# A hybrid attention / gated-linear-attention layer: the VectorE and ScalarE instructions of the side work pinned behind the projection product at which they are called

## The chip, the cores and the metric

The kernel runs on one core of one Trainium2 chip. Its engines are TensorE (PE, matrix products; its weight loads are listed as PEld), VectorE (DVE), ScalarE (ACT), GpSimd (POOL) and SyncE (SP, which here issues the loads). Each engine works through its own queue in the order in which the compiler placed the instructions. The metric is the device time of one execution in microseconds, the median of several runs; less is better.

## The reference

One layer (DEPTH 1, batch 1) over 256 latent tokens and 256 context tokens of width 2048, all in float32:

```python
mod_x = split(silu(c) @ w_mod + b_mod, 6);  mod_c = the same of c_ctx
proj = lambda h: project_heads(h, w_in, ...)        # 13,344 columns: qa ka va qb kb vb rb lrf lrb gate_a gate_b
qa, ka, va, qb, kb, vb, rb, gf, gb, gate_a, gate_b = proj(modulate(x, g_mix, mod_x[0], mod_x[1]))
... the same columns of the context, of which keys, values and decays are used
o_attn = windowed_attention(rope(qa), rope(ka), va, context keys and values, sink)   # 16 heads, 4 kv heads, |i-j| <= 128
sf, sb = gla_final_state of the context in both directions                           # GLA: 4 heads, dk 256, dv 512
o_gla  = latent_gla(qb, kb, vb, gf, gb, sf, sb)
x = x + mod_x[2] * merge_branches(o_attn, o_gla, rb, gate_a, gate_b, gla_norm, w_attn_o, w_gla_o, w_out)
x = x + mod_x[5] * conv_ffn(modulate(x, g_ffn, mod_x[3], mod_x[4]), w_up, conv_w, conv_b, w_down)   # D_FF 5632
```

GLA is a linear attention whose state decays per channel by gates made from low-rank columns of the input; it runs over the sequence forwards and backwards and starts from the end states of the context. merge_branches multiplies each branch with the sigmoid of its gate columns. conv_ffn is an up-projection, a depthwise convolution of width 3, SwiGLU, and a down-projection.

## The kernel before

**Products.** Every float32 weight is split in two float32r parts: `split` (L64 to 67) makes `hi` as a rounded copy on ACT and `lo = src - hi` on DVE. A projection is then three products, high x high, high x low and low x high. `proj_nat`, `proj_T` and `proj_pair` walk down the contraction in steps of two 128-row chunks. For each step they call `tick()`, fetch a weight tile of 256 x 512 (`wload`, a 512 KB load by SP into one of 7 buffers with the tag `raw`), split it (`wsplit`: ACT writes `whi`, DVE writes `wlo`, 3 buffers each, traced at high priority) and issue the step's products through `mm` (L73), which remembers the last one in `last[0]`. A step has 24 products where the context goes along (K, V, KA, VA), 12 where only the latent tokens do (QA, RB, gates, `w_attn_o`, `w_gla_o`, `w_out`, `w_down`), and in `proj_pair` (`w_up`) 8 of 512 and 8 of 256 columns.

**Stages.** The opening makes the modulation and the first blocks of Q, K and V, group by group of the contraction; there the order of PE, DVE and ACT is fixed to the program's by `in_order`. Then follow, left to the scheduler: K's second block and the V blocks with one GLA head each beside them, KA and VA (keys and values of the attention), QA four times with the attention of the previous group beside it, RB, the merge (gate columns, `w_attn_o`, `w_gla_o`), `w_out`, and two halves of `w_up` and `w_down`.

**Work beside the projections.** It is called from `tick()`, in three ways:

- `defer(n, fn)`: `fn` runs n + 1 ticks later; used for the transposes of a finished block (`turn`, `to_T`), `second_norm` and others.
- `beside`: a generator, stepped at a rate per tick. `gla_A(h, ...)` (rate 1.65) makes the decay sums (`segs`), and for each of 8 levels a decayed q and k (`q2`, `k2`: ACT exponentials L812 to 820, DVE multiplies L814 and L821, DVE sums L823 to 826), whose small products `pa` come one step later; at the end the context's part with `kf` and `kg` (L844 to 853) and two more steps. `attend(g, ...)` (rate 1.4) does scores, softmax and the product with V.
- `pace()`: background steps at `bg_rate`. After the opening these are the steps of `matvec`, which computes the other four parts of the modulation (`silu(c) @ w_mod`) on DVE: a step takes 256 rows of 512 columns of `w_mod` in a `raw` buffer and adds them, scaled by a column, to `macc` with two multiply-adds (L337, L339). At its call a step issues its own load, if that isn't done, and the next step's. There are 0.3 steps per tick beside the GLA heads, 1.6 in KA and VA, none in QA, 0.52 in RB and the merge, 0.4 in `w_out` and 0.45 in `w_up`.

**What orders this work.** The scheduler simulates the engines when it compiles and places an instruction in its engine's queue when its operands are done by that simulation, oldest call first, splits before all. The products and transposes of the side work have a lower limit beside that: `tick` sets `pin[0] = last[0]`, the last projection product issued, and `mm_b` and `turn_b` (L83, L86) pass their instruction through `after`:

```python
    def after(i):
        if pin[0] is not None:
            tc.add_manual_dep(i.ins, pin[0].name, mybir.DependencyInfo(
                mybir.DependencyClass.NoSync, mybir.DependencyReason.DATA), reason="place among the products")
        return i
```

A NoSync edge keeps the order of placing, without a semaphore. DVE, ACT, POOL and SP have no such limit: their side work is placed as soon as its operands and buffers allow.

Of the kernel before, what the change touches and what calls it, by code (L numbers as in the profile page):

```python
# [30 lines left out]
MODB = [(t, 1) for t in range(4)] + [(t, 2) for t in range(4, 16, 2)]  # L31
DFF = 5632
SCALE = HD ** -0.5


def layer_kernel(ctx, tc, A, out):
    nc = tc.nc
    V, S, G, PE = nc.vector, nc.scalar, nc.gpsimd, nc.tensor
# [36 lines left out]
    def after(i):  # L75

        if pin[0] is not None:
            tc.add_manual_dep(i.ins, pin[0].name, mybir.DependencyInfo(
                mybir.DependencyClass.NoSync, mybir.DependencyReason.DATA), reason="place among the products")
        return i  # L80

    def mm_b(*a, **k):
        return after(PE.matmul(*a, **k))  # L83

    def turn_b(*a):
        return after(PE.transpose(*a))  # L86
# [800 lines left out]
    def v_block(c0, name):  # L887
        vh, vl = M(name + "h", [P, 4, 512], F32R), M(name + "l", [P, 4, 512], F32R)
        proj_nat(w_in, 0, c0, ALL, h_xc, lambda i, b: split(vh[:, i, :], vl[:, i, :], b))
        return vh, vl  # L890
# [22 lines left out]
    def with_gla(h, kb, block):  # L913
        res = []
        beside[:] = [gla_A(h, kb, qbt, res), 1.65, 0.0]
        v = block()
        for _ in beside[0]:
            pass
        beside.clear()
        return res, v  # L920
# [6 lines left out]
    a, kb1 = with_gla(0, kbt, kb_block)  # L927
# [4 lines left out]
    for h in (1, 2, 3):  # L932
        a, v = with_gla(h, kb1 if h > 1 else kbt, lambda h=h: v_block(VB + h * 512, f"v{h}"))
# [77 lines left out]
    def attend(g, qT):  # L1011
# [3 lines left out]
        for t in range(2):  # L1015
# [14 lines left out]
            sk = sink[:, 4 * g:4 * g + 4]  # L1030
            V.scalar_tensor_tensor(mx, mx, SCALE, sk, op0=ALU.mult, op1=ALU.max)
            V.tensor_tensor(es, sk, mx, op=ALU.subtract)
            V.tensor_scalar(mx, mx, -1.0, None, op0=ALU.mult)
            S.activation(es, es, AF.Exp)
            for h in range(4):
                S.activation(sc[h], sc[h], AF.Exp, scale=SCALE, bias=mx[:, h:h + 1],  # L1036
                             accum_out=ds_[:, h:h + 1])
# [306 lines left out]
```

## Time and profile before

| | |
|---|---|
| median of 3 runs | 2018.4 us (2017.47 to 2019.22) |
| the profiled execution's own time | 2015.55 us |
| its span, first to last instruction | 2013.3 us |
| mean granted TensorE clock | 0.999 |
| HBM read | 413.48 MB |

Times in the profile are microseconds from the start of the span, unless marked ns. A row of a group gives line, engine, operation, the tiles as output<-inputs, the shapes, the count, then busy time, mean ns of one, and the idle time of the engine before them with what ended it. L73 is the projections' products, L83 and L86 the side work's products and transposes, L66 and L67 the two halves of a split, L106 the loads. A row of the waits reads: who waited, for whom, us in total, times, the longest. A row of the timeline reads: start, length, engine, line, operation, tiles, count, and in brackets the idle time before it. A matmul's end is modelled, and products overlap in the pipeline, so that their lengths add up to more than the time between their starts.

### The profile page before, as it was taken

What the parts mean: (1) busy time and instruction counts of PE and PEld (TensorE: products, weight loads), DVE (VectorE), ACT (ScalarE), POOL (GpSimd) and SP (SyncE); (2) the same over time, 40 slices, a digit from 0 to 9 for tenths busy, and PEclk for the clock granted to TensorE, in tenths of its full rate; (3) what the DMA queues carried; (4) which work ended last, traced back from release to release, by engine and by line L of the source; (5) the groups of instructions that cost most, each with busy time, mean ns of one, the idle gap of its engine ahead of it and who ended that gap; (6) DMA issues with size and microseconds to landing.
All of it is one profiled execution on the core that took longest, in us unless ns stands there. A gap on an engine that the chain in (4) does not pass through costs nothing.

```text
span 2013.3 us, 27564 instructions
## 1 busy us (share of the span) xinstructions
PE 1985.8 (99%) x10452; PEld 1649.7 (82%) x10452; DVE 1447.0 (72%) x2246; ACT 970.6 (48%) x1415; POOL 37.2 (2%) x56
## 2 busy tenths in 40 slices
PE   9999999999999999999999999999999999999998
PEld 7778888887777777887778888888888888888887
DVE  5656767887758888877776476899897455667754
ACT  5223565552345656444344445665555434555532
POOL 0001000001000000000000000000000000000000
PEclk9999999999999999999999999999999999999999
DMA  9876222346543456788887586588885655555563
GB/s 390 330 274 218 92 83 86 102 125 205 171 156 116 129 187 203 254 278 270 272 272 239 189 313 209 179 267 270 265 273 199 211 197 189 188 188 188 189 215 110
DMA packets 200437, 417.41 MB, mean 207 GB/s; under 512 B 13040, under 2 KB 13456, under 8 KB 195696
## 3 DMA queue, kind: packets, MB, share of 16 engines
q1 hardware_dynamic: 198816, 411.48, 61.3%
q0 software_dynamic: 1056, 4.08, 0.6%
q8 instruction: 82, 1.34, 0.3%
q14 instruction: 51, 0.42, 0.1%
q10 hardware_dynamic: 432, 0.09, 0.0%
HBM read 413.48 MB, written 2.11 MB: 206 GB/s over the span
## 4 chain that ended last, share of the span: by engine, by line
PE 58%; DMA 5%; DVE 3%; issue 1%; ACT 0%; DVEq 0%; ACTq 0%
PE acc L73 43%; PE accs L73 12%; DMA raw<-in_w_mod 5%; DVE macc L339 2%; DVE wlo L67 1%; PE poa L83 1%; PE pS L83 1%; PE ptp L86 1%; PE pto L86 0%; ACT whi L66 0%; PE ptx L86 0%; DVE s L1041 0%; ACT s L1036 0%; DVE macc L337 0%; PE ptq L86 0%
## 5 line engine op out<-in xcount | busy, mean ns | idle before, releaser
L66 ACT ACTIVATE whi<-raw 128x1024 fp32r<-128x1024 f32 x536 | 567.5, 1059 | 701.3 <-PE acc L73 493.7
L67 DVE TENSOR_TENSOR wlo<-raw,whi 128x1024 fp32r<-128x1024 f32 x536 | 653.7, 1223 | 294.9 <-ACT whi L66 269.1
L339 DVE SCALAR_TENSOR_TENSOR macc<-raw,ccol,macc 128x512 f32<-128x512 f32 x240 | 181.0, 754 | 104.5 <-DMA raw<-in_w_mod 101.1
L73 PE MATMUL acc<-h,whi 128*128 128x512 f32 x672 | 183.8, 395 | 0.0
L73 PE MATMUL accs<-h,whi 128*128 128x512 f32 x672 | 180.3, 390 | 0.0
L73 PEld LDWEIGHTS accs<-h,whi 128*128 128x128 f32 x672 | 126.2, 188 | 28.2
L73 PE MATMUL acc<-whi,ah 128*128 128x512 f32 x352 | 137.1, 389 | 0.0
L73 PE MATMUL acc<-whi,al 128*128 128x512 f32 x352 | 137.1, 389 | 0.0
L73 PE MATMUL acc<-whi,h00hi 128*128 128x512 f32 x336 | 134.1, 399 | 0.5 <-DVE val L67 0.5
L73 PE MATMUL acc<-whi,h01hi 128*128 128x512 f32 x336 | 133.6, 398 | 0.0
L73 PE MATMUL acc<-whi,h00lo 128*128 128x512 f32 x336 | 131.9, 393 | 0.0
L73 PE MATMUL acc<-whi,h01lo 128*128 128x512 f32 x336 | 131.7, 392 | 0.0
L73 PEld LDWEIGHTS acc<-h,whi 128*128 128x128 f32 x672 | 115.6, 190 | 15.1
L73 PEld LDWEIGHTS acc<-h,wlo 128*128 128x128 f32 x672 | 102.7, 189 | 13.1
L73 PE MATMUL accs<-h,wlo 128*128 128x256 f32 x672 | 108.0, 283 | 0.0
L73 PE MATMUL acc<-h,wlo 128*128 128x256 f32 x672 | 106.8, 282 | 0.0
L73 PE MATMUL acc<-wlo,ah 128*128 128x512 f32 x352 | 94.1, 389 | 0.0
L73 PE MATMUL acc<-wlo,h01hi 128*128 128x512 f32 x336 | 93.0, 395 | 0.8 <-DVE wlo L67 0.7
L73 PE MATMUL acc<-wlo,h00hi 128*128 128x512 f32 x336 | 93.5, 393 | 0.1
L73 PEld LDWEIGHTS accs<-h,wlo 128*128 128x128 f32 x672 | 92.7, 192 | 0.0
L73 PEld LDWEIGHTS acc<-wlo,ah 128*128 128x128 f32 x352 | 66.1, 188 | 13.7
L73 PEld LDWEIGHTS acc<-whi,ah 128*128 128x128 f32 x352 | 66.1, 188 | 13.7
(406 smaller groups left out, 3668.0 us busy)
## 6 DMA issues: line engine op xcount, KB each, us to landing
raw<-in_w_in SPq DMA_DIRECT2D x204, 512.0 KB, 4.3
raw<-in_w_up SPq DMA_DIRECT2D x184, 512.0 KB, 3.5
raw<-in_w_mod SPq DMA_DIRECT2D x128, 512.0 KB, 4.2
raw<-in_w_down SPq DMA_DIRECT2D x88, 512.0 KB, 3.6
mraw<-in_k_wm SPq DMA_DIRECT2D x32, 1024.0 KB, 8.7
raw<-in_w_attn_o SPq DMA_DIRECT2D x32, 512.0 KB, 5.1
raw<-in_w_gla_o SPq DMA_DIRECT2D x32, 512.0 KB, 4.7
raw<-in_w_out SPq DMA_DIRECT2D x32, 512.0 KB, 4.7
```

What stands on the lines that cost most here:

```text
L66: S.activation(hi, src, AF.Copy)
L67: V.tensor_tensor(lo, src, hi.bitcast(F32), op=ALU.subtract)
L73: last[0] = PE.matmul(*a, **k).ins
L83: return after(PE.matmul(*a, **k))
L86: return after(PE.transpose(*a))
L339: V.scalar_tensor_tensor(a[0], raw[:, k, :], vec[:, kt:kt + 1], a[0], op0=ALU.mult, op1=ALU.add)
```

## The change

`V` and `S`, by which the kernel calls VectorE and ScalarE, become wrappers that pass each instruction through `after`. Whatever is called inside `tick()` (deferred functions, the generators, the background steps) gets the edge to the last projection product; outside `tick()` `pin[0]` is None and nothing changes. So evacuations at the end of a projection, `wsplit`, and what is left of a generator after its block have no new edge. Loads by SP, POOL's instructions, and `nc.scalar.dma_start` have none either. No instruction is added or removed.

```diff
+class Placed:
+
+
+    def __init__(self, engine, place):
+        self.engine, self.place = engine, place
+
+    def __getattr__(self, name):
+        f = getattr(self.engine, name)
+
+        def call(*a, **k):
+            return self.place(f(*a, **k))
+
+        return call
+
+
 def layer_kernel(ctx, tc, A, out):
     nc = tc.nc
     V, S, G, PE = nc.vector, nc.scalar, nc.gpsimd, nc.tensor
...
         return i
+
+    V = Placed(V, after)
+    S = Placed(S, after)
 
     def mm_b(*a, **k):
         return after(PE.matmul(*a, **k))
```

## The prediction

> **What bounds the kernel now.** I read the page first (busy shares, the chain that ended last), then the windows of 50 us, then who waits for whom, then the timeline at the longest waits.
>
> ```profile
> span 2013.3 us, 27564 instructions
> ...
> PE 1985.8 (99%) x10452; PEld 1649.7 (82%) x10452; DVE 1447.0 (72%) x2246; ACT 970.6 (48%) x1415; POOL 37.2 (2%) x56
> ...
> PE acc L73 43%; PE accs L73 12%; DMA raw<-in_w_mod 5%; DVE macc L339 2%; DVE wlo L67 1%; PE poa L83 1%; PE pS L83 1%; PE ptp L86 1%; PE pto L86 0%; ACT whi L66 0%; PE ptx L86 0%; DVE s L1041 0%; ACT s L1036 0%; DVE macc L337 0%; PE ptq L86 0%
> ```
>
> TensorE is busy for 99% of the span, so no change to VectorE or ScalarE can win more than the places where a product has to wait. The chain names one foreign cause: loads of w_mod, their multiply-adds `macc`, and `wlo` behind them. Where that lies is seen in the windows (columns: stretch, length, busy time and count of PE, PEld, DVE, ACT, POOL, clock, DMA share, GB/s):
>
> ```profile
> 900.00:950.00 50.00, 47.56 (x212) 38.16 (x211) 37.34 (x49) 20.23 (x21) 0.00 (x0) 1.00 0.81 269
> 950.00:1000.00 50.00, 48.89 (x210) 38.37 (x209) 35.76 (x45) 19.03 (x19) 0.00 (x0) 1.00 0.83 277
> 1000.00:1050.00 50.00, 48.51 (x215) 38.65 (x214) 37.20 (x47) 20.23 (x21) 0.00 (x0) 1.00 0.80 265
> 1050.00:1100.00 50.00, 49.91 (x221) 40.23 (x220) 35.06 (x47) 20.08 (x20) 0.00 (x0) 1.00 0.75 254
> 1100.00:1150.00 50.00, 50.00 (x226) 41.38 (x225) 24.58 (x23) 21.27 (x22) 0.00 (x0) 1.00 0.58 190
> ```
>
> From 900 to 1100 us PE is idle 2.44 + 1.11 + 1.49 + 0.09 = 5.1 us; in the window after it, where `macc` has ended, not at all, at one product per 50 / 226 = 0.221 us. The waits (total us, times, longest):
>
> ```profile
> PE acc L73 <- DVE wlo L67: 4.7, 7, 1.6
> PE pa L83 <- DVE q L814: 3.0, 4, 0.9
> PE pa L83 <- DVE kf L852: 2.5, 4, 1.0
> PE po L83 <- DVE v3l L67: 2.5, 1, 2.5
> PE ptk L86 <- DVE sq L972: 1.9, 1, 1.9
> ...
> DVE macc L339 <- DMA raw<-in_w_mod: 101.1, 58, 3.6
> ...
> PEld acc L73 <- DVE wlo L67: 11.1, 15, 2.0
> ```
>
> VectorE stands still 101.1 us for w_mod rows that haven't landed, with `wlo` splits queued behind it. One case, on four engines (start, length):
>
> ```profile
> 925.52 0.37 SPq L106 DMA_DIRECT2D raw<-in_w_mod  x1
> ...
> 929.23 1.06 ACT L66 ACTIVATE whi<-raw 128x1024 fp32r<-128x1024 f32 x1 [1.66 <-PE acc L73]
> ...
> 930.74 1.54 DVE L339 SCALAR_TENSOR_TENSOR macc<-raw,ccol,macc 128x512 f32<-128x512 f32 x2 [2.85 <-DMA raw<-in_w_mod]
> ...
> 932.20 1.22 DVE L67 TENSOR_TENSOR wlo<-raw,whi 128x1024 fp32r<-128x1024 f32 x1
> ...
> 933.47 1.20 PE L73 MATMUL acc<-wlo,oh 128*128 128x512 f32 x4 [1.56 <-DVE wlo L67]
> ```
>
> The load is issued at 925.52 and its `macc` starts only at 930.74, 5.2 us later; VectorE idled 2.85 us for it, then spent 1.54, and the product waited 1.56 us for the `wlo` behind.
>
> **The change part by part.** Every V and S call made inside `tick()` gets a no-sync edge to the last projection product. Such an edge puts no wait on the chip; it only forbids the compiler to place the instruction in its engine's queue ahead of that product. Three kinds of work are touched.
>
> (1) `macc` (L337, L339) and its transposes. Nothing is added or removed; their places move back past the `wlo` splits of about two later chunks (the `whi`/`wlo` tiles have three buffers). How far ahead they run now: RB's weights and half a `matvec` step per tick share the 7 `raw` buffers, and each step runs as soon as its load lands. Held back, a step's load lands several ticks of 12 x 0.221 = 2.7 us before its place, against the 5.2 us above, so the 2.85 us kind of idle goes and `wlo` is late by 1.54 us of work at most, which its lead over PE covers. What is late next is PE itself. Size: the 7 gaps sum to 4.7 us, but a product is shown busy longer than its pace, so each wait hides a little more:
>
> ```profile
> L73 PE MATMUL acc<-whi,ah 128*128 128x512 f32 x352 | 137.1, 389 | 0.0
> ```
>
> 0.389 - 0.221 = 0.17 us per wait, over the 15 waits that the weight loads show: 4.7 + 15 x 0.17 = 7.2 us. Bounds: 4.7 from the gaps alone; from the counts, 4 x 226 - (212 + 210 + 215 + 221) = 46 products too few, 46 x 0.221 = 10.2 us (too much, as the windows differ in their small products). I take 7.2, since it is built on the waits themselves.
>
> [...]
>
> Two single stalls have the same cause. At the end of the fourth GLA head and in the attention:
>
> ```profile
> 464.27 2.49 DVE L339 SCALAR_TENSOR_TENSOR macc<-raw,ccol,macc 128x512 f32<-128x512 f32 x3
> ...
> 466.67 1.48 DVE L67 TENSOR_TENSOR wlo<-raw,whi 128x1024 fp32r<-128x1024 f32 x1
> ...
> 468.07 2.47 DVE L67 TENSOR_TENSOR v3l<-acc,v3h 128x512 fp32r<-128x512 f32 x4
> ...
> 468.80 0.50 PE L83 MATMUL po<-v3l,ats 128*128 128x512 f32 x1 [2.52 <-DVE v3l L67]
> ```
> ```profile
> 740.38 1.54 DVE L339 SCALAR_TENSOR_TENSOR macc<-raw,ccol,macc 128x512 f32<-128x512 f32 x2 [2.49 <-DMA raw<-in_w_mod]
> ...
> 742.58 0.50 PE L83 MATMUL poa<-ptl,vah 128*128 128x512 f32 x1 [0.88 <-DVE ptl L67]
> ```
>
> The first: three multiply-adds of steps that belong to KA's ticks stand ahead of the split that the `po` products need. KA's first steps are pinned to the last V product, so one or two may still stand there: between 0 and 2.5 us gone, I take 1.5. The second: 0.9 us gone with its DMA wait.
>
> Cost on SP's queue: a `raw` buffer with w_mod rows is now held until its tick, so later loads, which are issued in order, start later. In KA and VA (1.6 steps per tick of 24 x 0.221 = 5.3 us) the 7 buffers hold about 5 w_mod tiles and one or two weight chunks; in RB and the merge (0.52 steps per tick) two or three w_mod tiles and four chunks. One buffer's cycle, from the rows
>
> ```profile
> raw<-in_w_mod SPq DMA_DIRECT2D x128, 512.0 KB, 4.2
> ...
> L66 ACT ACTIVATE whi<-raw 128x1024 fp32r<-128x1024 f32 x536 | 567.5, 1059 | 701.3 <-PE acc L73 493.7
> L67 DVE TENSOR_TENSOR wlo<-raw,whi 128x1024 fp32r<-128x1024 f32 x536 | 653.7, 1223 | 294.9 <-ACT whi L66 269.1
> ```
>
> is 4.2 + 1.06 + 1.22 = 6.5 us: 1.2 buffers needed in VA, 2.4 in the merge. Covered, in VA barely.
>
> Cost on VectorE's queue in VA. The last KA/VA step runs at 526.77 to 535.69 now; its tick is VA's last, before `vah` at 567:
>
> ```profile
> 535.69 0.75 DVE L339 SCALAR_TENSOR_TENSOR macc<-raw,ccol,macc 128x512 f32<-128x512 f32 x1
> ...
> L66 ACT ACTIVATE vah<-acc x4: 576/592/610, 567.0 to 568.5; 128x512 fp32r<-128x512 f32 x4
> ...
> 500.00:550.00 50.00, 48.06 (x218) 38.71 (x217) 36.24 (x77) 16.22 (x28) 0.00 (x0) 1.00 0.56 179
> 550.00:600.00 50.00, 49.45 (x221) 40.33 (x220) 25.71 (x42) 20.27 (x28) 0.00 (x0) 1.00 0.46 140
> ```
>
> Some six ticks' steps, 6 x 1.6 x 1.5 = 14 us of VectorE, move into 530 to 567, where by these windows 28 to 49% of 37 us, 10 to 18 us, is free. Queued behind them are `val` and the key transposes, for which PE waits. I add 1.5 us; bounds 0 and 5 (three steps of 1.5 us ahead of `val`).
>
> (2) `gla_A`'s exponentials, multiplies and sums, which today may run a level ahead of their tick. They are now made in the tick whose products (or the next tick's) read them. PE's waits on them today are the eight above, 5.5 us. They may go (-5.5), or the other 4 x 7 = 28 level groups may wait likewise, 5.5 / 8 = 0.7 us each (+19.6). Today's groups already follow their operand closely without a gap:
>
> ```profile
> 308.76 0.69 DVE L821 TENSOR_TENSOR k<-k,kb 128x512 f32<-128x512 f32 x1
> ...
> 309.60 1.13 PE L83 MATMUL pa<-q,k 128*128 128x128 f32 x8
> ```
>
> (operand done 309.45, product 309.60, no idle), so I stay near zero: +1.5 us for two late groups.
>
> (3) All else at nothing. `attend`'s and the deferred turns' V and S work reads products that are pinned to the same tick already. In the opening each engine's order is fixed by hand. `second_norm` feeds `h2`, first read a block side later (8 ticks). POOL's `gc` sums and gate transfers follow pinned products' ACT work as before. The up stage shows no wait on `wlo` today: there `macc` waits are covered by 2 chunks' lead.
>
> Sum: -7.2 - 1.5 - 0.9 + 1.5 + 1.5 = -6.6 us: span 2013.3 to 2006.7, the profiled execution 2015.55 to 2008.95; that execution lies 2.85 us under the median, so the median goes from 2018.4 to 2011.8.
>
> **Rivals.** *Nothing measurable*: the edges bind only at compile time, and where VectorE's order keeps `macc` ahead of the same `wlo`, or costs (1) and (2) eat the gain, the time stays 2018.4. For it: all gains hang on some 17 waits. Against: 101 us of DMA wait in one queue should not survive a move of several ticks.
>
> *Operands just in time* (slower): without the level in hand each level's product is placed when the compiler thinks its operands are done, and the chip is 0.7 us late at all 28: +19.6 - 9.6 = +10.0, 2028.4. It decides from 14 late groups (9.6 / 0.7). Against it the row at 309.60; for it the eight waits, at the head's first and last groups.
>
> *Ring too short* (slower): every KA/VA chunk's load waits for held steps: 6.5 + 1.5 - 5.3 = 2.7 us a tick, 16 ticks, less two chunks in hand (10.6): +32.6, with the 8.1 us from elsewhere 2042.9. It decides when less than 1.2 buffers are left. [...]
>
> *More than counted*: counts' size and the eight waits too, -10.2 - 2.5 - 0.9 - 5.5 = -19.1: 1999.3.
>
> **How the numbers follow.** Forecast 0.48 (its own range 2007 to 2015), nothing 0.25, just in time 0.13, ring 0.06, more 0.08. A measurement of this kernel tells about 0.2% or 4 us from no change. Faster: 0.45 of the forecast's 0.48 + 0.08 = 0.53; same 0.25 + 0.03 = 0.28; slower 0.19. The range 2003 to 2026 leaves out "more", the ring and half of "just in time", 0.2 in all.
>
> **What would show it.** Right: `macc`'s wait for w_mod falls from 101 us to under 20; the `acc` from `wlo` row (4.7) all but goes; windows 900 to 1100 show 225 products each; the last w_mod `macc` of that stretch starts 20 us or more later than now. Wrong: the `pa` rows grow above 10 us, `whi` waits for weight loads, or VA's window shows PE idle before `vah`'s successors.

## The result and the profile after

| | before | after |
|---|---|---|
| median (runs) | 2017.93 us (2015.10 to 2019.22, 4) | 2004.20 us (2003.26 to 2004.61, 4) |
| the profiled execution's own time | 2015.55 us | 2004.46 us |
| its span | 2013.3 us | 2002.6 us |
| predicted | | 2011.8 us (2003 to 2026) |

The ratio is 0.9933, 95% interval 0.9916 to 0.995: faster by 0.7%, which is clear of the noise. The time lies at the lower end of the stated range and under the 2007 to 2015 us that the forecast had for itself, nearer to the rival "more than counted" (1999.3). The spans differ by 10.7 us, the medians by 13.7. The difference between the two is where the profiled execution of before lies among its own runs: 2.4 us under their median, in a spread of 4.1 us.

The page of the kernel after, its first lines and the chain by line. The wrapper now issues every VectorE and ScalarE instruction, so these all carry its line, L46; products of the projections are L88, those of the side work L101, turns L104.

```profile
span 2002.6 us, 27556 instructions
...
PE 1980.9 (99%) x10452; PEld 1651.1 (82%) x10452; DVE 1446.1 (72%) x2246; ACT 970.0 (48%) x1415; POOL 34.7 (2%) x56
...
PE acc L88 47%; PE accs L88 12%; PE pto L104 0%; PE ptx L104 0%; PE pcl L101 0%; DVE yd L46 0%; DVE wlo L46 0%; PE pr L101 0%; DVE u L46 0%; DVEq L1357 0%; DVE al L46 0%; DVE gcol L46 0%; PE pt_gate L104 0%; DVEq L46 0%
```

The loads of w_mod, 5% of the chain before, and `macc`, 2%, are gone from it. PE's busy share says nothing: 99% both times, and the same 10452 products. The windows say more (columns as before):

```profile
500.00:550.00 50.00, 46.54 (x210) 36.80 (x208) 38.86 (x83) 13.53 (x26) 0.00 (x0) 1.00 0.61 191
550.00:600.00 50.00, 49.08 (x215) 40.06 (x216) 37.00 (x56) 22.28 (x30) 0.00 (x0) 1.00 0.73 236
900.00:950.00 50.00, 50.00 (x227) 41.22 (x226) 40.77 (x52) 21.04 (x23) 0.00 (x0) 1.00 0.86 291
950.00:1000.00 50.00, 50.00 (x223) 40.91 (x222) 39.05 (x51) 20.39 (x21) 0.00 (x0) 1.00 0.82 279
1000.00:1050.00 50.00, 50.00 (x226) 41.13 (x225) 39.75 (x53) 20.89 (x22) 0.00 (x0) 1.00 0.85 291
1050.00:1100.00 50.00, 50.00 (x226) 41.12 (x225) 34.44 (x41) 20.95 (x23) 0.00 (x0) 1.00 0.73 253
```

From 900 to 1100 us PE has no idle time left, and 902 products stand where 858 stood. From 500 to 600, in VA, there are 425 where there were 439: this stage became slower. The waits, of all engines, and the group of `macc`:

```profile
ACT whi L46 <- DMA raw<-in_w_in: 72.4, 21, 6.7
ACT whi L46 <- DMA raw<-in_w_up: 42.8, 27, 3.6
...
PE pa L101 <- DVE kf L46: 2.8, 4, 0.9
...
PE pa L101 <- DVE q L46: 2.4, 4, 0.9
```
```profile
L46 DVE SCALAR_TENSOR_TENSOR macc<-raw,ccol,macc 128x512 f32<-128x512 f32 x240 | 179.7, 749 | 2.1
```

`macc` waits for no load any more (2.1 us of idle time before all 240 of them, against 104.5 us before, 101.1 of them behind loads). In its place the first half of a split, `whi`, waits for weights: 72.4 us for w_in and 42.8 us for w_up, two rows that before did not have. No row of `acc` behind `wlo` is left on PE.

Where the 10.7 us lie is read by counting the products of the projections (tiles acc, accs, acx) in both traces and comparing the start of the same product. Each cell is what a stretch became longer or shorter, in us; all experiments are set against the same profile of before:

| products (us in the trace before) | after | macc only | all but macc | resident | short | VA 0.8 | 0.45 | lead 2 | 6 buffers | lead 2, 0.8 | lead 4 | lead 12 | before, 6 |
|---|---|---|---|---|---|---|---|---|---|---|---|---|---|
| to the 1800th (428) | 0.0 | -1.3 | +1.0 | +8.9 | +0.7 | -0.1 | 0.0 | +0.1 | +2.3 | +1.0 | -0.5 | +0.1 | +3.4 |
| to the 2000th (494), end of the fourth head | -3.5 | +2.2 | -4.2 | -1.7 | +0.6 | -3.7 | -2.1 | -2.0 | -3.7 | -2.1 | -2.1 | -1.8 | +2.5 |
| to the 2400th (591), VA | +2.7 | +2.0 | -0.3 | -2.2 | +2.4 | -2.9 | +3.4 | -2.2 | +2.7 | -3.0 | -2.2 | +2.9 | -0.3 |
| to the 3400th (894), attention, RB | -0.6 | 0.0 | +0.4 | -0.5 | +1.6 | 0.0 | +2.9 | -1.6 | +6.5 | -0.2 | -0.9 | +5.6 | +2.8 |
| to the 4200th (1088), merge | -9.3 | -9.3 | -0.4 | -9.3 | -9.3 | -8.9 | -0.9 | -9.3 | +8.2 | -8.9 | -9.3 | -3.7 | -0.1 |
| to the last | 0.0 | 0.0 | +3.4 | 0.0 | 0.0 | +0.4 | +4.5 | 0.0 | +16.1 | +0.4 | 0.0 | 0.0 | +1.6 |
| sum | -10.7 | -6.3 | 0.0 | -4.9 | -4.0 | -15.2 | +7.8 | -15.1 | +32.2 | -12.7 | -15.0 | +3.2 | +9.9 |

One column is one execution. How far two executions of the same order lie apart is seen in three of them. The kernel with 0.45 steps has the instructions of before on PE, VectorE and ScalarE in the same order up to 717 us, and its stretches there still differ by -2.1 and +3.4 us. The kernels with all edges but `macc`'s and with twelve ticks ("lead 12") have the order of before throughout the merge (824 instructions on PE, 173 on VectorE, 79 on ScalarE), and their merges differ by -0.4 and -3.7 us. So a single cell of 2 or 3 us says little; what comes back in several kernels says more. The merge's -9.3 comes back to a tenth of a microsecond in five other kernels.

The case that the prediction showed at 925 us, now (start, length):

```profile
912.25 0.37 SPq L124 DMA_DIRECT2D raw<-in_w_mod  x1
...
925.87 1.23 DVE L46 TENSOR_TENSOR wlo<-raw,whi 128x1024 fp32r<-128x1024 f32 x1 [0.83 <-ACT whi L46]
927.01 1.53 DVE L46 SCALAR_TENSOR_TENSOR macc<-raw,ccol,macc 128x512 f32<-128x512 f32 x2
...
927.29 1.07 PE L88 MATMUL acc<-wlo,h01hi 128*128 128x512 f32 x4
```

`wlo` stands ahead of the two multiply-adds, which start without a wait, and the products behind `wlo` start without one. The second multiply-add is the first to read the load issued at 912.25, which landed at 915.79. Counted step by step, in the merge of before the first multiply-add of each of the 31 steps starts 0.0 to 0.8 us after its load has landed, and 28 of them have waited for it: VectorE comes to nearly every load before it is there. In the kernel after it is 9.6 to 17.2 us behind the landing (34 steps), and none waits.

### The profile page after: what moved, and what is told of

The parts are those of the page before. It is cut to its first block, busy times and chain, and to the rows that moved or that the text cites. A ratio compares the mean times of both kernels' runs of the same rounds, so it can differ in the third digit from the quotient of the medians.

```text
span 2002.6 us, 27556 instructions
## 1 busy us (share of the span) xinstructions
PE 1980.9 (99%) x10452; PEld 1651.1 (82%) x10452; DVE 1446.1 (72%) x2246; ACT 970.0 (48%) x1415; POOL 34.7 (2%) x56
## 4 chain that ended last, share of the span: by engine, by line
PE 60%; DVE 0%; DVEq 0%; issue 0%
PE acc L88 47%; PE accs L88 12%; PE pto L104 0%; PE ptx L104 0%; PE pcl L101 0%; DVE yd L46 0%; DVE wlo L46 0%; PE pr L101 0%; DVE u L46 0%; DVEq L1357 0%; DVE al L46 0%; DVE gcol L46 0%; PE pt_gate L104 0%; DVEq L46 0%
## 5 line engine op out<-in xcount | busy, mean ns | idle before, releaser
L46 ACT ACTIVATE whi<-raw 128x1024 fp32r<-128x1024 f32 x568 | 601.6, 1059 | 765.9 <-PE acc L88 455.8
L46 DVE TENSOR_TENSOR wlo<-raw,whi 128x1024 fp32r<-128x1024 f32 x568 | 694.5, 1224 | 383.9 <-ACT whi L46 353.6
L88 PE MATMUL acc<-h,whi 128*128 128x512 f32 x672 | 183.9, 395 | 0.0
L46 DVE SCALAR_TENSOR_TENSOR macc<-raw,ccol,macc 128x512 f32<-128x512 f32 x240 | 179.7, 749 | 2.1
L88 PE MATMUL accs<-h,whi 128*128 128x512 f32 x672 | 180.3, 390 | 0.0
L88 PEld LDWEIGHTS accs<-h,whi 128*128 128x128 f32 x672 | 126.2, 188 | 28.2
L88 PE MATMUL acc<-whi,ah 128*128 128x512 f32 x352 | 137.2, 390 | 0.0
L88 PE MATMUL acc<-whi,al 128*128 128x512 f32 x352 | 137.1, 389 | 0.0
L88 PE MATMUL acc<-whi,h00hi 128*128 128x512 f32 x336 | 134.3, 400 | 2.0 <-ACT y L46 1.4
L88 PE MATMUL acc<-whi,h01hi 128*128 128x512 f32 x336 | 133.8, 398 | 2.3 <-ACT whi L46 2.3
L88 PE MATMUL acc<-whi,h00lo 128*128 128x512 f32 x336 | 131.9, 393 | 0.0
L88 PE MATMUL acc<-whi,h01lo 128*128 128x512 f32 x336 | 131.6, 392 | 0.0
L88 PEld LDWEIGHTS acc<-h,whi 128*128 128x128 f32 x672 | 115.6, 190 | 15.1
L88 PEld LDWEIGHTS acc<-h,wlo 128*128 128x128 f32 x672 | 102.8, 189 | 13.1
L88 PE MATMUL accs<-h,wlo 128*128 128x256 f32 x672 | 108.0, 283 | 0.0
L88 PE MATMUL acc<-h,wlo 128*128 128x256 f32 x672 | 106.8, 282 | 0.0
L88 PE MATMUL acc<-wlo,ah 128*128 128x512 f32 x352 | 94.1, 389 | 0.0
L88 PE MATMUL acc<-wlo,h00hi 128*128 128x512 f32 x336 | 93.7, 394 | 0.0
L88 PEld LDWEIGHTS accs<-h,wlo 128*128 128x128 f32 x672 | 92.8, 192 | 0.0
L88 PE MATMUL acc<-wlo,h01hi 128*128 128x512 f32 x336 | 92.7, 393 | 0.0
L46 DVE SCALAR_TENSOR_TENSOR u<-us,cols,u 128x255 f32<-128x255 f32 x176 | 77.6, 478 | 0.5
L88 PEld LDWEIGHTS acc<-wlo,ah 128*128 128x128 f32 x352 | 66.1, 188 | 13.7
```

The lines of the kernel that those rows point to most:

```text
L46: return self.place(f(*a, **k))
L88: last[0] = PE.matmul(*a, **k).ins
```

## The experiments

The theory after the result: in the merge, `wlo` stood in VectorE's queue behind a `macc` whose load had not landed; places moved back end that. Open were which edges matter, whether the wait or the work of `macc` is the harm, and what VA's loss comes from.

**One part alone.** The edges on `matvec`'s four VectorE instructions only, on top of the kernel before:

```diff
-                    V.scalar_tensor_tensor(a[0], raw[:, k, :], vec[:, kt:kt + 1], a[0],
+                    after(V.scalar_tensor_tensor(a[0], raw[:, k, :], vec[:, kt:kt + 1], a[0],
...
-                V.tensor_reduce(rs, tr, op=ALU.add, axis=AX.X)
+                after(V.tensor_reduce(rs, tr, op=ALU.add, axis=AX.X))
```

> The kernel before, with the edge to the last product only on the VectorE instructions of matvec (multiply-adds, transpose, reduction). If the whole gain is matvec's (theory): span 2002.6 +- 1.5 us, as after: 9.3 us less between 900 and 1085 us, about 3.5 less at 450 to 475, about 2.8 more in VA. If the edges on the GLA heads' exponentials and multiplies had a part (rival), the span differs from 2002.6 by more than 2 us, with the difference between 200 and 470 us.

And the change without these, so with all other edges:

```diff
-                    V.scalar_tensor_tensor(a[0], raw[:, k, :], vec[:, kt:kt + 1], a[0],
+                    nc.vector.scalar_tensor_tensor(a[0], raw[:, k, :], vec[:, kt:kt + 1], a[0],
...
```

> The changed kernel without the edges on matvec's VectorE instructions. Theory: nothing happens, span 2013.3 +- 1.5 us, macc still waits about 100 us for w_mod loads, and the acc products wait about 4.7 us for wlo. Rival (edges on the GLA heads matter): 2 us or more to either side, found between 200 and 470 us.

Measured: the first 2007.81 us, ratio 0.9952 (0.9936 to 0.9968); the second 2013.34 us, 0.9981 (0.997 to 0.9992). The two ratios multiply to 0.9933, that of the change. The theory that all is `matvec`'s missed: the first kernel's span is 2007.0 us and not 2002.6. The second's span came out as said, 2013.3 us, but by luck, as -4.2 and +3.4 us cancel in it; its ten runs are faster than before by 0.2%. The merge's 9.3 us belong to `matvec`'s edges alone: with all others the waits stay as before:

```profile
DVE macc L357 <- DMA raw<-in_w_mod: 106.0, 61, 3.7
...
PE acc L88 <- DVE wlo L46: 8.2, 13, 2.3
```

The end of the fourth head goes the other way: -4.2 us without `matvec`'s edges, +2.2 with them alone. Its gain belongs to the edges on `gla_A`: the four kernels that hold `gla_A` to its own tick show -3.5 to -4.2 us there, and those without such edges, before among them, between -2.1 and +2.5. The size is therefore anything from 1.4 us up. Taking `macc` away from ahead of the split does not end the stall. The first `po` products, in the kernel with `matvec`'s edges alone, in the one without them, and in the kernel after:

```profile
460.83 1.03 PE L83 MATMUL pa<-q,kg 128*128 128x256 f32 x4
...
467.24 0.84 PE L83 MATMUL po<-v3h,ats 128*128 128x512 f32 x2 [1.97 <-ACT v3h L66]
```
```profile
465.03 1.03 PE L101 MATMUL pa<-q,kg 128*128 128x256 f32 x4
...
466.82 0.39 PE L101 MATMUL po<-v3h,ats 128*128 128x512 f32 x1
```
```profile
461.40 0.68 DVE L46 TENSOR_TENSOR v3l<-acc,v3h 128x512 fp32r<-128x512 f32 x1
...
464.30 1.03 PE L101 MATMUL pa<-q,kg 128*128 128x256 f32 x4
...
466.33 0.40 PE L101 MATMUL po<-v3h,ats 128*128 128x512 f32 x1
```

With `gla_A` held, the `pa` products of its context part (`kg`) stand 3.5 to 4.2 us later than with `matvec`'s edges alone, and one of the four `v3` splits (two in the second kernel) is made ahead of the weights' split (461.40), so `po` has operands at once.

**Wait or work.** In the kernel before, `macc` reads a constant tile that is always there; the loads, their count and the time on VectorE stay:

```diff
-                    V.scalar_tensor_tensor(a[0], raw[:, k, :], vec[:, kt:kt + 1], a[0],
+                    V.scalar_tensor_tensor(av, ov, vec[:, kt:kt + 1], av,
                                            op0=ALU.mult, op1=ALU.add)
```

> The kernel before, where matvec's multiply-adds read a tile that is always there instead of the loaded rows; the loads are still issued (the modulation's four later parts are thus not computed). No edges. VectorE's work and its size stay, the wait for the load goes. If the wait is what delays wlo: PE idle from 900 to 1100 us falls from 5.1 to under 1 us, span near 2004. If the 1.5 us of work ahead of wlo is what delays it: PE idle stays at 4 to 5 us.

And the reverse: it still waits for its load, but works on 32 of 512 columns:

```diff
-                    V.scalar_tensor_tensor(a[0], raw[:, k, :], vec[:, kt:kt + 1], a[0],
+                    V.scalar_tensor_tensor(a[0][:, 0:32], raw[:, k, 0:32], vec[:, kt:kt + 1], a[0][:, 0:32],
                                            op0=ALU.mult, op1=ALU.add)
```

> The kernel before, where matvec's multiply-adds cover 32 of 512 columns (the modulation's four later parts are thus not computed in full): they still wait for their load, but take about 0.1 us instead of 0.75. If the wait is what delays wlo: PE still idles 3 us or more from 900 to 1100 us. If the work is: under 1 us.

Measured: 2010.57 and 2011.07 us, one time each. Both free the merge wholly, PE 50.00 in each of the four windows, by the same 9.3 us. (The resident one loses 8.9 us in the opening, where a product waits 3.73 us for `kb`.) The short one does so while VectorE waits for w_mod longer than before in the whole kernel, and nearly as long in the merge (40.1 us against 45.1):

```profile
DVE macc L339 <- DMA raw<-in_w_mod: 136.1, 71, 6.0
```
```profile
900.00:950.00 50.00, 50.00 (x227) 41.21 (x226) 32.73 (x52) 21.28 (x22) 0.00 (x0) 1.00 0.88 293
...
1050.00:1100.00 50.00, 50.00 (x224) 41.18 (x223) 29.80 (x42) 20.67 (x21) 0.00 (x0) 1.00 0.68 223
```

So neither the wait nor the work is the harm by itself: `wlo`'s lead over PE covers each, and not both one after the other. The theory of the wait alone missed here. The short kernel is the firmer half of this: VectorE's order in its merge is nearly that of before (162 of 173 instructions match in sequence), while in the resident one, which has no load to wait for, the compiler orders the queue anew (103 of 173).

**Fewer steps.** The kernel before with 0.45 instead of 0.52 steps per tick in RB and the merge, to see whether the stall is set by the rate of the loads:

```diff
-    bg_rate[0] = 0.52
+    bg_rate[0] = 0.45
```

> The kernel before, without edges, with 0.45 matvec steps per tick in RB and the merge instead of 0.52. In the trace before, w_mod loads follow each other at about 6.1 us (986.64 - 918.15 over 11), each issued only after the previous step's macc and wlo; PE at full speed would call one every 2.84 / 0.52 = 5.5 us. If that closed loop bounds the merge (theory): at one every 2.84 / 0.45 = 6.3 us PE no longer waits, and most of the 9.3 us between 900 and 1085 goes, span 2004 to 2006. If each step just costs its own delay (rival): 9.3 x 0.45 / 0.52 = 8.0 us stay, span 2012.

Measured: 2020.93 us, ratio 1.0025 (1.0013 to 1.0037), where the theory had 2004 to 2006 us and the rival 2012. The waits did not shrink, and the trace shows +4.5 us after the merge. That the steps left over delay the stages behind is likely but not shown, as the kernel with all edges but `macc`'s, whose order there is nearly that of before, shows +3.4:

```profile
DVE macc L339 <- DMA raw<-in_w_mod: 127.4, 63, 5.1
...
PE acc L73 <- DVE wlo L67: 7.5, 11, 1.9
```

The theory of a loop closed through the buffers, which a lower rate would open, falls. What fits is that each step carries its own risk of a delay, wherever it is put: in this kernel's merge, too, 29 of 30 steps come to their load before it has landed.

**What VA's loss is.** Two cures of different kinds. Fewer held steps, 0.8 instead of 1.6 per tick in KA and VA:

```diff
-    bg_rate[0] = 1.6
+    bg_rate[0] = 0.8
```

> The changed kernel with 0.8 matvec steps per tick in KA and VA instead of 1.6 (the rest of the steps runs on in the merge at the same 0.52). If VA's 2.8 us come from held steps (buffers and VectorE's time): PE's waits there (whi 2.3, y 1.4 us) go, the span is 2002.6 - 2.8 = 1999.8 +- 1 us. If they come from the edges themselves or the evacuation of KA: unchanged, 2002.6 +- 1.

The same steps, held less long, by an edge to the projection product two ticks earlier:

```diff
+LEADT = 2
...
+    def after_early(i):
+        if pin[0] is not None and early[0] is not None:
+            tc.add_manual_dep(i.ins, early[0].name, mybir.DependencyInfo(
...
-    V = Placed(V, after)
-    S = Placed(S, after)
+    V = Placed(V, after_early)
+    S = Placed(S, after_early)
...
+        past.append(last[0])
         pin[0] = last[0]
+        early[0] = past[max(0, len(past) - 1 - LEADT)]
```

> The changed kernel with the VectorE and ScalarE edges on the projection product of two ticks earlier. If what counts is that macc is placed after its load has landed: the merge keeps its 9.3 us (the load is issued four to six ticks ahead), and VA loses less than 2.8 us, as buffers are freed two ticks sooner; span 2000 to 2003. If macc must stand behind the split of its own tick: half of the merge's waits return, 2007.

Measured: 2000.98 us, ratio 0.9922 (0.9907 to 0.9937), and 2000.03 us, 0.9918 (0.9902 to 0.9935). The first has a span of 1998.1 us, under the 1999.8 +- 1 that was expected. Both turn VA's +2.7 into a gain, -2.9 and -2.2. That +2.7 is no larger than what two executions of before differ by (the kernel with 0.45 steps has +3.4 there, with a 3.8 us wait of `ptk` for `sq`); but the change swaps that stall for another, and the medians point the same way, 3.2 and 4.2 us under the change's, though the intervals of the ratios overlap. The stall in the kernel after is a load that comes late:

```profile
525.14 0.37 SPq L124 DMA_DIRECT2D raw<-in_w_in  x1
531.40 2.91 SPq L124 DMA_DIRECT2D raw<-in_w_mod  x2
538.28 0.37 SPq L124 DMA_DIRECT2D raw<-in_w_in  x1
```
```profile
541.69 1.06 ACT L46 ACTIVATE whi<-raw 128x1024 fp32r<-128x1024 f32 x1 [5.46 <-DMA raw<-in_w_in]
...
542.79 0.50 PE L88 MATMUL acc<-whi,h01hi 128*128 128x512 f32 x1 [1.27 <-ACT whi L46]
```

The weights' load is issued at 538.28, 13.1 us after the weights' load before it and behind two loads of w_mod, for which a buffer has to come free. From 480 to 592 us SP waits 24.9 us for a `macc` to free one, against 15.2 in before, 17.0 with two ticks and 2.8 with 0.8 steps. With the edge two ticks earlier the 72.4 us that `whi` waits for w_in are 8.3, and PE's window is full:

```profile
ACT whi L47 <- DMA raw<-in_w_in: 8.3, 5, 2.1
```
```profile
500.00:550.00 50.00, 50.00 (x230) 40.59 (x229) 43.46 (x88) 16.21 (x29) 0.00 (x0) 1.00 0.65 211
550.00:600.00 50.00, 49.07 (x218) 39.69 (x217) 32.98 (x52) 21.15 (x29) 0.00 (x0) 1.00 0.61 197
```

VectorE is busier there (43.46 us) than in the kernel after (38.86), and PE doesn't mind: VA's loss is weight loads that come late, and not VectorE's work.

**The ring.** The change with 6 `raw` buffers, and the kernel before with 6:

```diff
-wr = pool(name="wr", bufs=7)
+wr = pool(name="wr", bufs=6)
```

> The changed kernel with 6 raw buffers instead of 7. If the ring is what VA lacks: VA's cost grows from 2.8 to more than 5 us, with whi waiting on w_in loads for well over 72 us in all, while the merge (2.4 buffers needed for weights) stays without waits; span 2005 to 2010. If VectorE's time is what VA lacks: 2002.6 +- 1.

> The kernel before with 6 raw buffers instead of 7. If holding the steps is what makes the ring short (the kernel with the change lost 43 us at 6 buffers), the kernel before, which frees a buffer as soon as its load has landed, loses less than half of that: 2018 to 2038 us, with whi waiting on loads of w_up, where no step runs, as long as there. Rival, that 6 buffers are too few for the weights by themselves: 2055 to 2065 us, whi waiting on loads over 200 us.

Measured, one time each: the change 2047.22 us, 43 us above its own median with 7; the kernel before 2025.46 us, beside a median of 2016.85. In the change the weights wait for loads in every stage with steps, and PE with them:

```profile
ACT whi L46 <- DMA raw<-in_w_in: 133.5, 58, 7.5
ACT whi L46 <- DMA raw<-in_w_up: 80.5, 48, 4.9
...
PE acc L88 <- ACT whi L46: 26.9, 30, 2.8
```

In the kernel before with 6 the longest waits for loads are still those of `macc`, not of `whi`:

```profile
DVE macc L339 <- DMA raw<-in_w_mod: 108.1, 61, 3.9
...
ACT whi L66 <- DMA raw<-in_w_out: 6.2, 3, 4.3
```

So 6 buffers are nearly enough for the work itself; it is holding the steps that needs the seventh. (I had expected `whi` of before to wait for w_up as long as in the change, as if no step ran there; it waits 2.9 us for it against 80.5, and 71.6 of these fall before 1540 us, where steps still run.) My size for the change with 6 (2005 to 2010 us) was far too small, and its place was wrong: VA's cost did not grow, +2.7 us as with 7, with `whi` waiting 38.8 us for loads there against 43.7. The merge, which was to stay without waits, lost 17.5 us against the change with 7, and the stages behind it 16.1. Why a buffer less does no harm in VA is left open.

**How late is late enough.** The edge to the product four and twelve ticks earlier (10.6 and 32 us ahead in the merge), and the two cures of VA together:

> The change with edges on the product four ticks earlier (10.6 us ahead in the merge, 21 us in VA). If an instruction does harm only when it is queued before its load has landed: a load takes 4 to 7 us to land, and it is issued only when a buffer is free, so the merge keeps most of its 9.3 us and the time is 2000 to 2003 us, with macc waiting on loads 10 to 40 us. Rival, that the two ticks were the whole margin: waits of acc on wlo come back, 2 to 5 us, and 2004 to 2008 us.

> The change with edges on the product twelve ticks earlier (32 us in the merge, 64 us in VA), where the edges hardly bind. If place alone matters, the merge goes back to the kernel before: macc waits on loads 80 to 100 us, acc on wlo 3 to 5 us, 3 to 9 us of the merge's gain gone, 2009 to 2014 us; the end of the fourth head loses its 3.5 us too. Rival, that the merge's gain comes from some other effect of the edges (another order of the splits): it stays, 2000 to 2004 us.

> The change with edges on the product two ticks earlier and 0.8 instead of 1.6 steps of matvec per tick in KA and VA. Theory that both cures mend one and the same cost (VectorE too full of held steps between 500 and 570 us, 2.8 us): nothing more than the better of the two, 2000 +- 1 us, ratio 0.992. Rival, that they mend two things (lateness of each step and the load of the queue): 1997 to 1998.5 us.

Measured: four ticks 2001.61 us, ratio 0.9924 (0.991 to 0.9938); twelve ticks 2017.38 us, 1.0005 (0.9993 to 1.0017), above the 2009 to 2014 expected; both cures 2002.37 us, 0.9927 (0.9913 to 0.9941), 1.4 us above the upper end of what was expected. At four ticks `macc` still waits for no load (I had expected 10 to 40 us); in the merge its steps start 4.2 to 9.3 us after their load has landed, and 7.1 to 13.3 us with two ticks. At twelve the kernel is in the merge the one before again, in its order and its waits:

```profile
DVE macc L47 <- DMA raw<-in_w_mod: 103.4, 63, 3.6
...
PE acc L90 <- DVE wlo L47: 3.5, 5, 1.0
```
```profile
950.00:1000.00 50.00, 47.88 (x207) 37.71 (x206) 35.61 (x45) 18.72 (x20) 0.00 (x0) 1.00 0.81 270
1000.00:1050.00 50.00, 48.66 (x218) 39.28 (x217) 36.81 (x48) 20.62 (x22) 0.00 (x0) 1.00 0.82 276
```

So it is the place that counts, not some other effect of the edges. Both cures together bring nothing over one, as if they mended the same cost. Of the versions, the edge two ticks earlier has the lowest median, 4.2 us under the change's, and the traces put 4.4 us between the two, 4.9 of them in VA with smaller differences of both signs elsewhere; the intervals of the ratios overlap, with the change's too.

The place seems to decide the spread too. The ten runs at twelve ticks lie between 2012.37 and 2023.88 us, the kernel before between 2013.08 and 2019.64 (15 runs); with two ticks four runs lie between 1999.94 and 2000.23, and none of the six kernels that hold `macc` spreads over more than 1.9 us, in four or five runs each.

## Why the prediction was right in its sign and short in its size

It said -6.6 us of span; the traces show -10.7. That the sum is not further off is in part luck, as several terms missed with opposite signs. Term by term, from the table above:

- *The merge, -7.2 said, -9.3 measured.* The mechanism was right: `matvec`'s edges alone give it, at twelve ticks the merge has the order and the waits of before again, and of the signs named, `macc`'s wait and the row of `acc` behind `wlo` went as said, and PE's windows show the 225 products. Too small was the term for what a wait hides, 15 x 0.17 us. PE's idle time in those windows fell by 5.1 us, while 44 more products stand in them, 44 x 0.221 = 9.7 us. The count, which I had set aside as too much (10.2), was the better end: the 5.1 us of idle time stand beside 9.3 us of delay.
- *The 20 us by which `macc` would move back.* As the sign was worded, it did not show: the last one of the merge starts at 1073.3 us instead of 1067.8, 5.5 us later. But the projection itself runs some 10 us ahead by then, and the last one of the merge isn't the same step. Of the 272 instructions that write `macc`, the 161st stands beside the 3763rd projection product before and beside the 3853rd after; 90 products at 0.221 us are 20 us. Against the products the move was as forecast.
- *A sign of being wrong came too*: `whi` waits for weight loads, 72.4 us for w_in and 42.8 for w_up. In VA PE waits for it; in the merge and behind it PE does not.
- *The end of the fourth head, -1.5 said, -3.5 measured, for the wrong reason.* I blamed the three `macc` at 464.27, which stand in the queue ahead of `v3l`. The two kernels with one part alone show that it is the order of `pa` and the `v3` splits: with `macc` away `po` still waits, and with `macc` there but two `v3` splits ahead of it `po` does not. Part of the size is the clock, below: another execution of the order of before lost 2.1 us less there.
- *VA, +1.5 said, +2.7 measured.* The sum for VectorE's load pointed at the wrong resource: the kernel with two ticks has more of VectorE's work there and no such stall. What failed is the step that put the cost on SP's queue at nothing ("Covered, in VA barely"): weight loads are issued late there, behind loads of w_mod whose buffers are held. The 1.2 buffers that I had counted as covered "barely" were the right line to press, though counting buffers doesn't explain it all: VA lost the same with 6 of them, and the 43 us lie in the stages behind. So the rival of the short ring did not happen, though it was nearer than its 0.06 said. With 6 buffers `acc` waits 30 times for `whi`, 26.9 us in all.
- *`gla_A`'s operands, +1.5 said, about 0 measured*: `pa` waits 5.2 us where it waited 5.5, and the stretch to 428 us is unchanged. The rival of operands just in time did not happen.
- *The stall at 742.58, -0.9 said*: that stretch gained 0.6. The wait of `poa` for `ptl` (1.1 us) is gone, and one of `pto` for `sr` (1.2 us) is new.

The forecast 2011.8 then also stood on the median; the rest of the distance to 2004.2 is where the profiled execution of before lay in a spread that the change itself removes.

Left open: why VA lost no more with 6 buffers than with 7, what gives the kernel before with fewer steps its new waits, and why the change with 6 buffers lost 16 us after the merge.

## What to carry to other kernels

VectorE took its queue in order here, so an instruction placed ahead of its load held up what stood behind it: in before `wlo`, whose `whi` ended at 930.29, started at 932.20, behind a `macc` whose load let it start only at 930.74. The lead of `wlo` covered the wait alone and the work alone, and with both the merge took 9.3 us more; hold background work until its data are surely there. Holding cost buffers (with 6 instead of 7 the change took 43 us more): find by one run with a buffer less how near the ring is to its end, and hold no longer than needed (here two to four ticks earlier were as good as the exact place or better, twelve were worth nothing). Where an engine is nearly always busy, as PE here with 99%, price a stall by the products missing from a window (9.7 us here, against 9.3 measured), not by the idle time that the profile shows (5.1).

## What the hardware showed that I had not expected

After the 2.52 us in which PE stood still up to 468.80, its granted clock fell, from 1.00 to 0.50 at 469.77. The products that follow start 0.42 us apart in before and 0.23 us apart in the kernel after:

```profile
470.31 0.63 PE L83 MATMUL po<-v3h,atc 128*128 128x512 f32 x1
470.73 0.63 PE L83 MATMUL po<-v3l,atc 128*128 128x512 f32 x1
```
```profile
469.25 0.39 PE L101 MATMUL po<-v3h,atc 128*128 128x512 f32 x1
469.48 0.40 PE L101 MATMUL po<-v3l,atc 128*128 128x512 f32 x1
```

Some eight products at 0.2 us more are 1.6 us, so by this estimate the stall cost about 4 us and not the 2.5 that the row of the wait shows. The kernel with 0.45 steps, whose order is the same here, waited 2.00 us; its clock stayed at 1.00 from 460 to 480 us, and its stretch is 2.1 us shorter.

In these traces the length of a wait does not decide this alone. With twelve ticks the clock fell after waits of 3.29 and 2.36 us and not after one of 2.31; with 0.45 steps it fell after one of 1.91 us, and with 6 buffers it stayed after one of 2.8.

What sorts the cases below is where the wait lies. In before the clock is at 0.50 for 3.413 us, from 469.77 to 473.18; it falls again at 2012.59, 451.0 such lengths behind 473.18. Cut into stretches of that length, counted from where the clock fell (with twelve ticks 812.63), before and the kernel with twelve ticks show (columns as in the prediction):

```profile
466.36:469.77 3.41, 0.97 (x4) 0.84 (x5) 3.41 (x5) 0.60 (x2) 3.21 (x6) 1.00 0.81 248
469.77:473.18 3.41, 3.41 (x9) 2.67 (x9) 3.30 (x6) 0.07 (x1) 0.00 (x0) 0.50 0.61 225
```
```profile
464.46:467.87 3.41, 1.96 (x9) 1.12 (x7) 3.34 (x4) 2.63 (x5) 3.41 (x5) 1.00 0.91 299
467.87:471.29 3.42, 2.56 (x11) 2.12 (x12) 3.38 (x7) 0.00 (x0) 1.64 (x5) 1.00 0.85 264
809.21:812.63 3.42, 1.06 (x9) 0.83 (x9) 3.42 (x5) 0.86 (x2) 0.00 (x0) 1.00 0.40 110
812.63:816.04 3.41, 3.41 (x11) 2.73 (x10) 3.33 (x6) 0.88 (x2) 0.00 (x0) 0.50 0.46 144
```

In before PE is idle for 2.44 of the 3.41 us ahead of the fall, and the next stretch runs at half the clock. With twelve ticks the 2.31 us wait falls into two stretches, 1.45 and 0.86 us idle, and the clock stays; the 2.36 us wait falls into one, and the clock halves. In before, too, the wait of `ptk` for `sq`, 1.94 us up to 532.61, falls into two, 0.55 and 1.40 us idle, and the clock stays. Of all such stretches of before and after, behind the first 60 us and ahead of the last 15, only the one with 2.44 us idle ends in a fall; in the others PE idles 1.56 us or less, by the modelled ends of the products. So here a wait of 2.00 us kept the clock, and one of 2.52 cost about 4 us by the estimate above, which can be part of why executions of one order differ. That the clock goes by such stretches in general is not shown by these few.
